# Sums of squares of attention heads: GpSimd's sum over partitions in place of matmuls with ones

## The chip, the cores and the metric

The kernel runs on one core of a Trainium2 chip. A core has five engines with a queue of instructions each: TensorE (PE in the profile, with its weight loads as PEld), VectorE (DVE), ScalarE (ACT), GpSimd (POOL) and SyncE (SP), which issues most of the transfers. Each engine works through its own queue in order and waits on semaphores for the others. SBUF is the memory on the chip, in 128 partitions; TensorE writes its results to PSUM. The metric is the device time of one execution in microseconds (us), the lower the better.

## The reference

One inference step of one layer, on 512 frames of a new stream (prompt) and 64 frames of a running stream with 512 cached frames. All is float32. Cut to what the change touches:

```python
def hybrid_layer(x, k_past, v_past, conv_past, g_norm1, w_in, g_q, g_k, ...):
    hn = rmsnorm(x, g_norm1)
    proj = hn @ w_in                        # D_MODEL = 2048
    q, k, v, gb, gc, hc = jnp.split(proj, ...)
    q = rmsnorm(q.reshape(B, T, N_HEADS, HEAD_DIM), g_q)    # 8 heads x 128 channels
    k = rmsnorm(k.reshape(B, T, N_HEADS, HEAD_DIM), g_k)
    ...
    o_attn = stick_breaking_blocks(q, k_all, v_all, P)
    ...                                     # short gated convolution
    mix = jnp.concatenate([rmsnorm(o_attn, g_attn_out), rmsnorm(o_conv, g_conv_out)], axis=-1)
    x = x + mix @ w_out
    ...                                     # second norm, gated FFN (5632 wide), residual

def stick_breaking(q, k, v, q_pos, k_pos):
    z = jnp.einsum('bqhd,bkhd->bhqk', q, k) / math.sqrt(HEAD_DIM)
    mask = (k_pos[None, :] < q_pos[:, None])[None, None]
    log_1mb = jnp.where(mask, jax.nn.log_sigmoid(-z), 0.0)
    after = lax.cumsum(log_1mb, axis=3, reverse=True) - log_1mb
    w = jnp.where(mask, jnp.exp(jax.nn.log_sigmoid(z) + after), 0.0)
    return jnp.einsum('bhqk,bkhd->bqhd', w, v)
```

`rmsnorm` divides by the root of the mean square. For q and k that mean goes over the 128 channels of one head.

## The kernel before

Channels lie on the partitions and the 576 frames on the free axis, worked on in two halves of 288. A float32 product is made of three fast products: each operand is split into a high part (a copy in the fast type, by ScalarE) and a low part (the difference, by VectorE; `split`, L220 to L222). A projection of 128 columns is 2 halves x 16 steps x 3 matmuls of 128x288.

The time is spent in four stages: the start (x is turned, up to about 45 us), the eight heads (to about 455 us), the convolution groups and the output projection, and the FFN, which takes most. In the stage of the heads each head has three projections (q, k, v), and the attention of the head before is fitted between their steps. The order on TensorE is written out by hand: generators are put on a heap (`Pipeline`), every step of a product is one tick, and `yield n` means "n ticks later". In the heads SP's order is by hand too; VectorE, ScalarE and GpSimd get theirs from a planner, which works with costs of its own.

`norm_evac` (L618) is the normalization of one head's q or k. `evac` runs as soon as a half of the projection lies in PSUM: VectorE scales it to `E` (L636), ScalarE squares it to `sq` (L639), and both split the squares into two parts (L221, L222). 13 ticks later (16 for k; 10 and more in head 0) `rest` lets TensorE multiply both parts by a matrix of ones: `channel_sums` (L467), two matmuls of 128x288 (L469, L470), which give `ss`, in each partition the sum over all partitions, in a PSUM bank called misc. `rsqrt_mean` (L455) makes the reciprocal root of it: `ms` (L460, VectorE reads `ss`), logarithm and exponential by ScalarE (L461, L462), three instructions of VectorE for a step of refinement (L463 to L465). L628 gives `qf` or `kf`, which is split to `qh`, `ql`, `kh`, `kl`. `attend` (L663) starts 15 ticks after the `rest` of k's last half, with the scores (L679, L682) in the banks `z`; then softplus, the mask, the sums of the blocks, and later the products with triangular ones (L725 to L740) and with v (L749). `cz` (L765 to L768) and `os` (L779) are the same for the cached part.

GpSimd does small work beside it: the product with the 0/1 mask `m01` (L691) or `s01` (L754), two additions of blocks per head (L694, L699), one copy and three additions for the cached part (L758, L760), the addition of a head's squares to `acc_a` (L509), and the low part of one weight (L175). In the first output stage it forms differences for `head_forms` (L557) and issues the stores of `mix` (L524).

Of the kernel before, what the change touches and what calls it, by code (L numbers as in the profile page):

```python
# [3 lines left out]

# [6 lines left out]
F32 = mybir.dt.float32  # L11
F32R = mybir.dt.float32r
AF = mybir.ActivationFunctionType
ALU = mybir.AluOpType
PSUM = bass.MemoryType.PSUM

P = 128
TP = 512
TS = 64
# [75 lines left out]
def tile_hybrid_stream_step(  # L95
# [88 lines left out]
    def split_weight(lo_eng):  # L184
        raw = raws[len(ready)]
        n = specs[len(ready)][1] * specs[len(ready)][2]
        hi, lo = weight_split(len(ready))
        for a in range(0, n, 1024):
            weight_parts(raw, hi, lo, a, a + 1024, lo_eng)
# [3 lines left out]
    def next_weight():  # L193
        i = pos[0]
        pos[0] += 1
        end = first_out if i < first_out else first_block
        while len(raws) < min(i + 2, end):
            load_weight()
        while len(ready) < min(i + 2, end):
            split_weight(nc.gpsimd if i == 2 else nc.vector)  # L200
        while len(raws) < min(i + 3, end):
            load_weight()
        out = ready[i]
        ready[i] = None
        return out
# [18 lines left out]
    def parts(name):  # L224
        t = tmp.tile([P, 2, HALF], F32R, tag="hl", name=name)
        return t[:, 0], t[:, 1]
# [273 lines left out]
            else:  # L500
                defer.append((evac, ps, a, b))

    def add_squares(acc, src, first):
        if first:
            nc.scalar.activation(out=acc, in_=src, func=AF.Square)
        else:
            sq = tmp.tile([P, HALF], F32, tag="sq", name="sqm")
            nc.scalar.activation(out=sq, in_=src, func=AF.Square)
            nc.gpsimd.tensor_tensor(out=acc, in0=acc, in1=sq, op=ALU.add)  # L509

    turns = {}

# [105 lines left out]
    def norm_evac(name, gcol, dst_f, dst_hi, dst_lo, first, after=None):  # L618
        E = t1.tile([P, T], F32, tag="E", name=f"E{name}", bufs=2)

        def rest(a, b, sh, sl):
            if first:
                lags[0] += 4
            yield 6 + lags[0] if first else 16 if after else 13
            ss = channel_sums(sh, sl, a, b, "ss")
            r = tmp.tile([P, HALF], F32, tag="r", name="r")
            rsqrt_mean(r, ss, P, HALF)
            nc.vector.scalar_tensor_tensor(out=dst_f[:, a:b], in0=E[:, a:b], scalar=gcol, in1=r,  # L628
                                           op0=ALU.mult, op1=ALU.mult)
            e = min(b, TP)  # L630
            split(dst_hi[:, a:e], dst_lo[:, a:e], dst_f[:, a:e])
            if after and b == T:
                pipe.spawn(after)

        def evac(ps, a, b):
            nc.vector.tensor_tensor(out=E[:, a:b], in0=ps, in1=R1[:, a:b], op=ALU.mult)  # L636
            sq = tmp.tile([P, HALF], F32, tag="sq", name="sq")
            sh, sl = parts("sq")
            nc.scalar.activation(out=sq, in_=E[:, a:b], func=AF.Square)  # L639
            split(sh, sl, sq)  # L640
            pipe.spawn(rest(a, b, sh, sl))

        return evac

# [14 lines left out]
        nc.vector.scalar_tensor_tensor(out=dst, in0=ps, scalar=0.0, in1=scratch, op0=ALU.max, op1=ALU.add)  # L659

    kw = dict(start=False, skip_group_check=True)

    def attend(h, st):  # L663
        yield 15 + (9 if h == 0 else 0)
# [19 lines left out]
        for b in (2, 1, 0):  # L684
            parts = (2, 3) if b == 2 else (b,)
            w = full[b]
            for i in parts:
                scores(i)
            softplus(pr[b][:, :w], z[b][:, :w], pr[b][:, :w])
            for i in parts:  # L690
                nc.gpsimd.tensor_tensor(out=pb[i][:, :P], in0=pb[i][:, :P], in1=m01, op=ALU.mult)  # L691
            split(ph[b][:, : width[b]], pl[b][:, : width[b]], pr[b][:, : width[b]])
            if b == 2:
                nc.gpsimd.tensor_tensor(out=pb[2][:, P:], in0=pb[2][:, P:], in1=pb[3], op=ALU.add)  # L694
                s1h = t1.tile([P, 256], F32R, tag="s1h", name="s1h")
                s1l = t1.tile([P, 256], F32R, tag="s1l", name="s1l")
                split(s1h, s1l, pb[2])
            if b == 1:
                nc.gpsimd.tensor_tensor(out=pb[1][:, P:], in0=pb[1][:, P:], in1=pb[2], op=ALU.add)  # L699
                s0h = t1.tile([P, 384], F32R, tag="s0h", name="s0h")  # L700
                s0l = t1.tile([P, 384], F32R, tag="s0l", name="s0l")
                split(s0h, s0l, pb[1])
# [48 lines left out]

        sp = t1.tile([P, T], F32, tag="pr0", name="sp")
        softplus(sp[:, :320], zc, sp[:, :320])
        nc.gpsimd.tensor_tensor(out=sp[:, 256:320], in0=sp[:, 256:320], in1=s01, op=ALU.mult)  # L754
        sh = t1.tile([P, T], F32R, tag="ph0", name="sph")
        sl = t1.tile([P, T], F32R, tag="pl0", name="spl")
        sums = sp[:, 320:]
        nc.gpsimd.tensor_copy(sums[:, 192:256], sp[:, 256:320])  # L758
        for b in (2, 1, 0):
            nc.gpsimd.tensor_tensor(out=sums[:, b * TS : (b + 1) * TS], in0=sums[:, (b + 1) * TS : (b + 2) * TS],  # L760
                                    in1=sp[:, (b + 1) * TS : (b + 2) * TS], op=ALU.add)
        split(sh, sl, sp)
        yield 18
# [16 lines left out]
        nc.scalar.copy(out=o_attn[h][:, TP:], in_=os_[:, TS:P])  # L780
        for a, b in HALVES:
            yield 3
            add_squares(acc_a[:, a:b], o_attn[h][:, a:b], h == 0)

    def values(h, st, Ev):
        yield 5
# [831 lines left out]
    acc = {}  # L1618
# [226 lines left out]
```

## Time and profile before

| what | us |
|---|---|
| median of 3 runs | 2382.36 (2382.0 to 2385.2) |
| profiled execution, first to last instruction | 2383.4 |
| TensorE busy in it | 2361.4 (99%) |
| VectorE busy | 1919.3 (81%) |
| ScalarE busy | 1172.1 (49%) |
| GpSimd busy | 295.2 (12%) |

The page gives the profiled execution no other time than its span, which lies within the range of the runs. Times inside a profile count from the span's start. In the lines below, `L212 PE MATMUL pj<-x,whi` is an instruction of line 212 on TensorE that writes `pj` and reads `x` and `whi`. A row of the timeline begins with start and duration; behind it stands, in brackets, how long the engine was idle before and what released it. A row of groups by form gives busy time, mean nanoseconds of one, and the idle time ahead of the group. A row of waits gives the total, the number of times and the longest. Matmuls overlap in the engine, so the starts of neighbours tell what one of them costs, not its duration. Some matmul records can be missing.

### The profile page before, as it was taken

What the parts mean: (1) busy time and instruction counts of PE and PEld (TensorE: products, weight loads), DVE (VectorE), ACT (ScalarE), POOL (GpSimd) and SP (SyncE); (2) the same over time, 40 slices, a digit from 0 to 9 for tenths busy, and PEclk for the clock granted to TensorE, in tenths of its full rate; (3) what the DMA queues carried; (4) which work ended last, traced back from release to release, by engine and by line L of the source; (5) the groups of instructions that cost most, each with busy time, mean ns of one, the idle gap of its engine ahead of it and who ended that gap; (6) DMA issues with size and microseconds to landing.
All of it is one profiled execution on the core that took longest, in us unless ns stands there. A gap on an engine that the chain in (4) does not pass through costs nothing.

```text
span 2383.4 us, 44109 instructions
## 1 busy us (share of the span) xinstructions
PE 2361.4 (99%) x17765; PEld 2349.5 (99%) x17765; DVE 1919.3 (81%) x2884; ACT 1172.1 (49%) x2107; POOL 295.2 (12%) x386
## 2 busy tenths in 40 slices
PE   8999999999999999999999999999999999999999
PEld 8999999999999999999999999999999999999999
DVE  7767776688887899888888888888888777887876
ACT  6666665444444555444444444444444444444444
POOL 1111111242111130000000000000000002431211
PEclk9999999999999999999999999999999999999999
DMA  8354433584367745444444444444444936886642
GB/s 257 117 152 142 144 112 96 184 285 127 109 216 199 217 155 177 151 125 147 152 131 143 150 137 140 147 144 134 146 147 133 355 116 207 221 231 198 202 132 81
DMA packets 512260, 390.76 MB, mean 164 GB/s; under 512 B 11838, under 2 KB 501176, under 8 KB 512056
## 3 DMA queue, kind: packets, MB, share of 16 engines
q1 hardware_dynamic: 502712, 371.40, 48.8%
q0 software_dynamic: 8624, 16.22, 3.3%
q8 instruction: 139, 2.28, 0.4%
q14 instruction: 65, 0.53, 0.1%
q10 hardware_dynamic: 720, 0.33, 0.0%
HBM read 298.82 MB, written 89.08 MB: 163 GB/s over the span
## 4 chain that ended last, share of the span: by engine, by line
PE 88%; DVE 5%; DMA 3%; ACT 2%; issue 1%; POOL 0%; SPq 0%; ACTq 0%; DVEq 0%; POOLq 0%
PE psy L1529 34%; PE psw L1529 17%; PE pj L212 11%; PE psx L1529 9%; PE psy L1033 5%; PE pjo L212 4%; PE psw L1033 3%; PE psx L1033 1%; DMA raw_a<-in_w_out_dram 1%; DMA o_ob<-xt_dram 1%; DVE whl L1005 1%; PE z L682 1%; PE po L749 0%; DMA raw_a<-in_w_down_dram 0%; DMA raw_a<-in_w_in_dram 0%
## 5 line engine op out<-in xcount | busy, mean ns | idle before, releaser
L1529 PE MATMUL psy<-h_s,whl 128*128 128x288 f32 x2787 | 411.4, 294 | 0.3 <-ACT part L1539 0.3
L212 PE MATMUL pj<-x,whi 128*128 128x288 f32 x1856 | 398.2, 299 | 0.3 <-DVE x L355 0.3
L1529 PEld LDWEIGHTS psy<-h_s,whl 128*128 128x128 f32 x2787 | 383.5, 188 | 0.6 <-ACT part L1539 0.6
L222 DVE TENSOR_TENSOR whl<-raw_a,whl 128x1024 fp32r<-128x1024 f32 (+4 forms) x296 | 323.1, 1092 | 59.1 <-ACT whl L221 58.3
L1529 PE MATMUL psw<-t,whl 128*128 128x288 f32 x2400 | 348.1, 295 | 0.0
L1529 PEld LDWEIGHTS psw<-t,whl 128*128 128x128 f32 x2400 | 327.7, 188 | 0.0
L221 ACT CAST whl<-raw_a 128x1024 fp32r<-128x1024 f32 (+4 forms) x296 | 267.8, 906 | 114.5 <-issue 35.4
L212 PEld LDWEIGHTS pj<-x,whi 128*128 128x128 f32 x1856 | 306.6, 189 | 1.0 <-DVE x L355 0.6
L212 PE MATMUL pj<-x,wlo 128*128 128x288 f32 x928 | 274.2, 295 | 0.1
L222 DVE TENSOR_TENSOR whl<-raw_b,whl 128x1024 fp32r<-128x1024 f32 (+5 forms) x190 | 200.6, 1056 | 70.4 <-ACT whl L221 69.2
L221 ACT CAST whl<-raw_b 128x1024 fp32r<-128x1024 f32 (+5 forms) x190 | 165.2, 872 | 169.1 <-issue 72.8
L1539 ACT COPY part<-psy 128x288 f32<-128x288 f32 x242 | 96.4, 398 | 282.8 <-PE psy L1529 281.3
L1529 PE MATMUL psy<-b22m,whl 128*128 128x288 f32 x1212 | 182.7, 294 | 0.4 <-ACT part L1539 0.4
L1529 PE MATMUL psy<-t2t,whl 128*128 128x288 f32 x1212 | 183.0, 294 | 0.0
L212 PEld LDWEIGHTS pj<-x,wlo 128*128 128x128 f32 x928 | 174.9, 188 | 0.7 <-DVE wlo L422 0.3
L1529 PE MATMUL psx<-h_s,whl 128*128 128x288 f32 x1185 | 173.5, 294 | 0.0
L1529 PEld LDWEIGHTS psy<-b22m,whl 128*128 128x128 f32 x1212 | 168.0, 188 | 0.7 <-ACT part L1539 0.7
L1529 PEld LDWEIGHTS psy<-t2t,whl 128*128 128x128 f32 x1212 | 168.2, 188 | 0.2 <-DVE whl L222 0.2
L1529 PEld LDWEIGHTS psx<-h_s,whl 128*128 128x128 f32 x1185 | 162.6, 188 | 0.0
L221 ACT CAST whl<-s 128x1024 fp32r<-128x1024 f32 (+5 forms) x81 | 72.3, 892 | 101.5 <-PE psw L1529 101.4
L1308 POOL DMA_DIRECT2D hid_dram<-form x3 | 2.2, 750 | 947.2 <-DVE form L222 947.2
L1529 PE MATMUL psy<-t,whl 128*128 128x288 f32 x576 | 107.6, 296 | 0.0
(483 smaller groups left out, 4446.7 us busy)
## 6 DMA issues: line engine op xcount, KB each, us to landing
hid_dram<-form SPq DMA_DIRECT2D x147, 288.0 KB, 2.3
raw_a<-in_w_in_dram SPq DMA_DIRECT2D x41, 1024.0 KB, 6.5
raw_a<-in_w_gate_dram SPq DMA_DIRECT2D x22, 1024.0 KB, 6.0
raw_a<-in_w_up_dram SPq DMA_DIRECT2D x22, 1024.0 KB, 5.7
raw_b<-in_w_gate_dram SPq DMA_DIRECT2D x22, 1024.0 KB, 6.6
raw_b<-in_w_up_dram SPq DMA_DIRECT2D x22, 1024.0 KB, 7.6
h_s<-hid_dram SPq DMA_DIRECT2D x10, 2016.0 KB, 11.6
raw_a<-in_w_out_dram SPq DMA_DIRECT2D x16, 1024.0 KB, 5.4
```

Source lines behind the costliest of these rows:

```text
L212: mm(ps, w_[:, k, csl], x_, start=(k == 0 and n == 0), stop=(k == nk - 1 and n == 2))
L221: nc.scalar.copy(out=hi, in_=src)
L222: (lo_eng or nc.vector).tensor_tensor(out=lo, in0=src, in1=hi.bitcast(F32), op=ALU.subtract)
L682: mm(zb[i], a_[:, kk], b_[:, q0:TP], start=(n == 0), stop=False, skip_group_check=True)
L1005: tt(out=whl[:, 1], in0=src, in1=whl[:, 0].bitcast(F32), op=ALU.subtract)
L1033: mm(ps, whl[:, w_, j, :], x_, start=(start and j == 0 and q == 0), stop=(j == m - 1 and q == 2), skip_group_check=True)
L1308: q.dma_start(out=hid_dram[fp][2 * n - 2 : 2 * n].rearrange("f p t -> p f t"), in_=t.bitcast(F32))
L1529: mm(ps, whl[:, w_, j, :], x_, start=(start and j == 0 and q == 0), stop=(j == len(xs_) - 1 and q == 2), skip_group_check=True)
L1539: nc.scalar.copy(out=t, in_=st["y"])
```

## The change

Four things are changed, all but one in the stage of the heads.

1. `norm_evac` no longer splits the squares and no longer multiplies by ones. `evac` gives the squares, whole, to GpSimd's `partition_all_reduce`, which writes the sum over the 128 partitions to all of them, in SBUF; `rest` reads it there. The result lies in the buffer (tag `hl`) that the split squares had. The other sums by `channel_sums` (the attention's and the convolution's output norm, the second norm) stay matmuls.
2. The products with the masks become selections by position (`affine_select`) on GpSimd: `later_queries`. For the cached part a `memset` of 64 partitions follows, since `s01` was zero there too.
3. The additions of blocks, of the cached part's sums and of the heads' squares go from GpSimd to VectorE; those of the convolution's squares stay.
4. One weight's low part goes from GpSimd to VectorE.

Counted over the program, TensorE has 64 matmuls less, ScalarE 32 casts less, VectorE 32 subtractions less and 48 other instructions more, and GpSimd 32 sums over partitions, 40 selections and 8 memsets more in place of 88 two-input operations. GpSimd's queue also holds two more special instructions, which switch the code that its cores have loaded: one behind `rst` (L440), ahead of the first sum, and one ahead of the first difference of `head_forms` (L557), behind two stores of `mix`. SP has as many instructions as before.

```diff
-            split_weight(nc.gpsimd if i == 2 else nc.vector)
+            split_weight(nc.vector)
...
-    def add_squares(acc, src, first):
+    def add_squares(acc, src, first, eng=nc.gpsimd):
...
-            nc.gpsimd.tensor_tensor(out=acc, in0=acc, in1=sq, op=ALU.add)
+            eng.tensor_tensor(out=acc, in0=acc, in1=sq, op=ALU.add)
...
-        def rest(a, b, sh, sl):
+        def rest(a, b, ss):
...
-            ss = channel_sums(sh, sl, a, b, "ss")
...
             sq = tmp.tile([P, HALF], F32, tag="sq", name="sq")
-            sh, sl = parts("sq")
             nc.scalar.activation(out=sq, in_=E[:, a:b], func=AF.Square)
-            split(sh, sl, sq)
-            pipe.spawn(rest(a, b, sh, sl))
+            ss = tmp.tile([P, HALF], F32, tag="hl", name="ss")
+            nc.gpsimd.partition_all_reduce(ss, sq, P, bass_isa.ReduceOp.add)
+            pipe.spawn(rest(a, b, ss))
...
+    def later_queries(t, base):
+
+        nc.gpsimd.affine_select(out=t, in_=t, compare_op=ALU.is_ge, fill=0.0, base=base,
+                                pattern=[[1, t.shape[1]]], channel_multiplier=-1)
...
-                nc.gpsimd.tensor_tensor(out=pb[i][:, :P], in0=pb[i][:, :P], in1=m01, op=ALU.mult)
+                later_queries(pb[i][:, :P], -1)
...
-                nc.gpsimd.tensor_tensor(out=pb[2][:, P:], in0=pb[2][:, P:], in1=pb[3], op=ALU.add)
+                nc.vector.tensor_tensor(out=pb[2][:, P:], in0=pb[2][:, P:], in1=pb[3], op=ALU.add)
...
-                nc.gpsimd.tensor_tensor(out=pb[1][:, P:], in0=pb[1][:, P:], in1=pb[2], op=ALU.add)
+                nc.vector.tensor_tensor(out=pb[1][:, P:], in0=pb[1][:, P:], in1=pb[2], op=ALU.add)
...
-        nc.gpsimd.tensor_tensor(out=sp[:, 256:320], in0=sp[:, 256:320], in1=s01, op=ALU.mult)
+        later_queries(sp[:, 256:320], TS - 1)
+        nc.gpsimd.memset(sp[:TS, 256:320], 0.0)
...
-            nc.gpsimd.tensor_tensor(out=sums[:, b * TS : (b + 1) * TS], in0=sums[:, (b + 1) * TS : (b + 2) * TS],
+            nc.vector.tensor_tensor(out=sums[:, b * TS : (b + 1) * TS], in0=sums[:, (b + 1) * TS : (b + 2) * TS],
...
-            add_squares(acc_a[:, a:b], o_attn[h][:, a:b], h == 0)
+            add_squares(acc_a[:, a:b], o_attn[h][:, a:b], h == 0, nc.vector)
```

More of the change, by code (lines that the diff above doesn't have):

```diff
@@ L5 @@
 import concourse.bass as bass
+import concourse.bass_isa as bass_isa
 import concourse.tile as tile
```

## The prediction

> **What bounds the kernel now.** I read the head of the page and the chain first, then a window over steady heads, then the two matmuls that go, and then who waits for whom there.
>
> ```profile
> span 2383.4 us, 44109 instructions
> PE 2361.4 (99%) x17765; PEld 2349.5 (99%) x17765; DVE 1919.3 (81%) x2884; ACT 1172.1 (49%) x2107; POOL 295.2 (12%) x386
> ...
> PE 88%; DVE 5%; DMA 3%; ACT 2%; issue 1%; POOL 0%; SPq 0%; ACTq 0%; DVEq 0%; POOLq 0%
> ...
> 90.00:405.00 315.00, 314.02 (x2336) 310.17 (x2336) 225.83 (x442) 191.70 (x413) 48.63 (x92) 1.00 0.42 128
> ...
> 114.07 1.22 PE z L682 x6
> ...
> 413.54 1.23 PE z L682 x6
> ```
>
> TensorE holds 88% of the chain and is busy 314.02 of 315 us in the window (its columns: PE, weight load, VectorE, ScalarE, GpSimd, then clock and DMA). The clock is 1.00, so nothing is to be had there. The two score rows lie six heads apart: (413.54 - 114.07)/6 = 49.9 us per head. Per head VectorE is busy 225.83 x 49.9/315 = 35.8 us and GpSimd 48.63 x 49.9/315 = 7.7 us. So a matmul taken out of TensorE's row is worth its issue interval, as long as VectorE's 14.1 idle us per head are not used up.
>
> ```profile
> 105.74 0.29 PE L469 MATMUL ss<-sq,oner 128*128 128x288 f32 x1
> 105.87 0.29 PE L470 MATMUL ss<-sq,oner 128*128 128x288 f32 x1
> 106.00 0.30 PE L212 MATMUL pj<-x,whi 128*128 128x288 f32 x1
> ...
> PE z L682 <- ACT kh L221: 1.6, 3, 0.8
> PE kc L800 <- ACT zc L710: 1.0, 1, 1.0
> PE kc L800 <- DVE ms L460: 0.5, 1, 0.5
> PE ss L469 <- DVE ms L460: 0.3, 1, 0.3
> ```
>
> A matmul is shown as 0.29 us but the next one starts 0.13 us later: the pair takes 106.00 - 105.74 = 0.26 us of the row. Between 40 and 480 us TensorE waits for other engines 3.4 us in all: only the scores' wait for kh, in 3 heads of 8, repeats.
>
> **Part 1: the matmuls go.** 8 heads x (q, k) x 2 halves = 32 pairs at 0.262 us (0.131 each) = 8.4 us off TensorE. The wait of ss for a free bank (0.3) and of kc behind it (0.5) hang on the bank that ss held: they go, 0.8 us. What is late next is the scores; I leave their 1.6 us. The gain passes to the end if what follows is tied to the heads' end, not to the clock:
>
> ```profile
> 457.72 0.14 PE ssg L469
> ...
> 518.31 8.63 DMA raw_a<-in_w_in_dram
> ```
>
> After the last head the chain goes from ssg through VectorE's scaling to this load, each released by the one before, so it moves forward as a block.
>
> **Part 2: the splits and the additions.** The rows of 47 to 420 us, by form:
>
> ```profile
> L222 DVE TENSOR_TENSOR sq<-sq 128x288 fp32r<-128x288 f32 x32 | 17.8, 559 | 3.7 <-ACT sq L221 3.5
> ...
> L606 DVE TENSOR_TENSOR o_ob<-o_ob 128x288 f32<-128x288 f32 x8 | 3.6, 454 | 0.1
> ...
> L719 DVE SCALAR_TENSOR_TENSOR z<-z,acA 128x128 f32<-128x128 f32 x28 | 8.3, 295 | 7.0 <-PE z L728 6.2 <-PE z L734 0.6
> ...
> L222 DVE TENSOR_TENSOR pl<-pr,ph 128x256 fp32r<-128x256 f32 x15 | 6.7, 448 | 1.5 <-ACT ph L221 1.5
> ...
> L772 DVE SCALAR_TENSOR_TENSOR ws<-ws,acA 128x64 f32<-128x64 f32 x7 | 1.5, 214 | 0.0
> ...
> L175 DVE TENSOR_TENSOR wlo<-raw_a,whi 128x1024 fp32r<-128x1024 f32 x43 | 52.4, 1225 | 6.8 <-ACT whi L174 6.4
> ```
>
> VectorE loses 17.8 us of subtractions. It gains 14 x 0.454 = 6.4 (the head squares' additions), 8 x 0.295 = 2.4 and 8 x 0.448 = 3.6 (block sums), 24 x 0.214 = 5.1 (the cached part's sums) and 2 x 1.225 = 2.5 (a weight's low part): 20.0, so +2.2 in all, or 0.3 per head, beside 14.1 idle. ScalarE loses 32 casts and gains nothing. Both hidden; without cover the 2.2 us would be the price. GpSimd's masks become one-input selections; the two rows of such at the start are first below, and an addition of GpSimd follows that part 3 needs:
>
> ```profile
> L246 POOL TENSOR_SCALAR_AFFINE_SELECT acA<-acA 128x128 f32<-128x128 f32 x1 | 0.3, 292 | 0.0
> ...
> L251 POOL TENSOR_SCALAR_AFFINE_SELECT acA<-acA 128x64 f32<-128x64 f32 x1 | 0.2, 239 | 0.0
> ...
> L509 POOL TENSOR_TENSOR acc_a<-acc_a,sqm 128x288 f32<-128x288 f32 x14 | 12.5, 890 | 85.4 <-ACT sqm L508 85.4
> ```
>
> **Part 3: the sum over partitions, X us each.** No row shows it. Below: it is a sum over a 128x288 tile, so hardly under the same engine's addition of that shape, 0.89 (last row). A tree over 128 partitions has 7 halvings: 7 x 0.89 = 6.2. I take the geometric middle, the root of 0.89 x 6.2 = 2.35. Far end: one partition after another; a column of one pass costs (292 - 239)/64 = 0.83 ns, so 288 x 128 x 0.83 = 30.6 us. Its place in a head:
>
> ```profile
> 201.27 0.44 ACT L639 ACTIVATE sq<-Ek 128x288 f32<-128x288 f32 x1 [0.34 <-DVE Ek L636]
> ...
> 208.33 0.45 DVE L460 TENSOR_SCALAR ms<-ss 128x288 f32<-128x288 f32 x1
> ...
> 212.21 0.39 DVE L222 TENSOR_TENSOR kl<-kf,kh 128x224 fp32r<-128x224 f32 x1 [0.45 <-ACT kh L221]
> ...
> 213.50 0.28 PE L682 MATMUL z<-qh,kh 128*128 128x256 f32 x1
> ```
>
> This is the head's last half, the one that the scores wait for. The squares are ready at 201.71, and ms used its sum only at 208.33: 6.6 us cover X = 2.35 here. The new wait is at ms on VectorE. Behind it in the changed order stand, in head 0, both subtractions of a weight that is used one projection later, elsewhere the rest of the normalization and x's sums; in a head in which ms stands straight after Eq, VectorE stands still for about 0.45 + 2.35 us, out of 14.1. On GpSimd the cached part's mask may stand behind a sum and be X late, but its three additions leave GpSimd. SP's DMAs are the same in number; POOL's two mix stores come ahead of the second code switch.
>
> **Part 4: two switches of GpSimd's code.** The changed order holds two more special instructions: after rst, and before the head forms' first subtraction. Bounds: between the ends of the memset and the start of the selection below lay one such instruction and 0.08 us; above, a transfer of 1 MB takes 6.5 us to land.
>
> ```profile
> 0.81 0.20 POOL masks.py:197 MEMSET ident<- 128x128 f32 x1 [0.29 <-POOLq L1832]
> ...
> 1.09 0.29 POOL masks.py:199 TENSOR_SCALAR_AFFINE_SELECT ident<-ident 128x128 f32<-128x128 f32 x1
> ...
> raw_a<-in_w_in_dram SPq DMA_DIRECT2D x41, 1024.0 KB, 6.5
> ...
> 38.78 1.21 POOL L440 TENSOR_TENSOR rst<-ssr,nhalf 128x5 f32<-128x5 f32 x1 [12.09 <-DVE ssr L438]
> ...
> 47.02 0.81 ACT L639 ACTIVATE sq<-Eq 128x288 f32<-128x288 f32 x2 [6.86 <-DVE Eq L636]
> ...
> 465.06 0.74 POOL L524 DMA_DIRECT2D mix_dram<-mx  x1 [7.33 <-DVE mx L522]
> ...
> 468.66 1.78 POOL L557 TENSOR_TENSOR o_oa<-o_oa 128x288 f32<-128x288 f32 x2 [2.86 <-DVE hf L222]
> ...
> 476.18 2.29 POOL L557 TENSOR_TENSOR o_oa<-o_oa 128x288 f32<-128x288 f32 x2 [1.50 <-DVE hf L222]
> ...
> 485.75 2.24 POOL L557 TENSOR_TENSOR o_ob<-o_ob 128x288 f32<-128x288 f32 x2 [3.04 <-DVE hf L222]
> ```
>
> The first has 47.4 - 40.0 = 7.4 us of cover, more than 6.5. The second has 2.9; the upper bound would start the subtractions 3.6 late, which GpSimd's idle 1.50 and 3.04 later in that chain take up. I take 0 for both and keep 3.6 for the range.
>
> **Sum.** -8.4 - 0.8 = -9.2 us. The page gives the profiled execution no time but its span, 2383.4, which is 1.0 above the runs' median of 2382.4; nothing else lies around it. So 2374.2 against the span, 2373.2 against the median. Changes within 0.2%, 4.8 us (2377.6 to 2387.2), are what a measurement of this kernel can hardly tell from none.
>
> **Rival 1, slower: VectorE is shut out while GpSimd sums.**
>
> ```profile
> 49.51 5.00 POOL L175 TENSOR_TENSOR wlo<-raw_a,whi 128x1024 fp32r<-128x1024 f32 x2 [9.53 <-ACT whi L174]
> ...
> 50.99 0.46 DVE L460 TENSOR_SCALAR ms<-ss 128x288 f32<-128x288 f32 x1 [1.98 <-PE ss L470]
> ...
> 52.44 2.38 DVE L463 TENSOR_TENSOR t<-y 128x288 f32<-128x288 f32 x1 [0.20 <-ACT y L462]
> ```
>
> While GpSimd's two additions run (49.51 to 54.51), VectorE's product of two SBUF inputs lasts 2.38 us and ends 0.3 after them; the one that reads PSUM takes its usual 0.46. If the sums shut VectorE out for all of X, a head needs 35.8 + 0.3 + 4X of VectorE against TensorE's 49.9 - 1.05 = 48.9. It decides from X = 3.2. At 2.35 a head needs 45.5 and the gain stands; at 4 it needs 52.1, so 8 x 2.2 = 17.6 us more than before: 2400; at 6.2, 60.9: +88, 2470. Against it: products that read PSUM go on, and 7.7 us of GpSimd's present two-input work shut VectorE out already and shrink to some 2. The Trainium skill (SBUF — State Buffer, section "SBUF: two separate sides") says that the pair of ports is an exclusive lock, taken for the whole instruction; the row above agrees, and no run yet shows whether a sum over partitions holds it to its end. Chance 0.20, for X between 3.2 and 6.2.
>
> **Rival 2, much slower: the sums walk the partitions one by one and GpSimd is the bound.** From X = 12 on (48.9/4) GpSimd alone exceeds the head; at the far end 4 x 30.6 = 122 us per head, 8 x 72.5 = +580: 2962. The Trainium skill (GPSIMD Engine Reference, section 3.2, Cross-partition) has 247.7 us for a reduction along partitions of a 128x2048 tile; scaled to 288 columns that would be an estimate of 34.8 us each. Against it: it is another instruction than the one used. No row decides; 0.05.
>
> **Rival 3, no change: the scores eat the gain.** If kh and kl are ready no earlier than now, TensorE reaches the scores 0.52 us sooner per head (two pairs lie between) and waits for it: 8 x 0.52 = 4.2 lost, and 3.6 by the second switch. Gain 9.2 - 7.8 = 1.4: 2381. For it: kl ends at 212.60, 0.9 before the scores, and three heads wait already. Against it: the 6.6 us of cover above. 0.14.
>
> **Chances.** Forecast 0.56 (faster; own range 2371, with the scores' 1.6 us as well, to 2377). No change 0.14. Slower 0.30: rival 1 0.20, rival 2 0.05, and 0.05 for orders of VectorE that stall on ms for more than the idle time. The range goes from 2371 to 2400, rival 1 at X = 4; rival 2 and the upper half of rival 1 stay out.
>
> **What would show it.** Right: 64 fewer matmuls on ss, per-head distance of the score rows near 48.9, sums over partitions under 3.2 us, ms waiting little, TensorE still at 99%. Wrong: VectorE rows of two SBUF inputs that last as long as the sum beside them, TensorE waiting for kh or for whi/wlo in each head, a sum over 3.2 us, GpSimd idle before the first sum until after 48 us, or the head forms' subtractions starting late.

## The result, and the profile after

The changed kernel takes 2394.43 us (median of 5 runs, 2394.02 to 2400.26) against 2384.19 (2382.0 to 2385.94) for the kernel before in the same series: a ratio of 1.0045, 95% interval 1.0034 to 1.0057. It is 10 us (0.45%) slower, where 9 us less was forecast; the range of 2371 to 2400 holds it, on the other side of zero. (A correction to the count under "The change": VectorE has 56 other instructions more, not 48, and GpSimd has lost 96 two-input operations, not 88.)

The head of the page and its chain, of the changed kernel:

```profile
span 2392.7 us, 43956 instructions
PE 2360.4 (99%) x17701; PEld 2348.3 (98%) x17701; DVE 1917.9 (80%) x2908; ACT 1166.2 (49%) x2075; POOL 325.2 (14%) x370
...
PE 86%; DVE 5%; DMA 3%; ACT 2%; POOL 2%; issue 1%; SPq 0%; ACTq 0%; POOLq 0%; DVEq 0%
```

The 64 matmuls are gone, and still TensorE's busy time fell by 1.0 us instead of 8.4, while the span grew by 9.3. So TensorE both waits and runs slower than before. Where it waits, from 20 to 620 us (us in total, times, longest), in the changed kernel:

```profile
PE os L785 <- issue: 7.2, 4, 2.7
PE psy L1039 <- ACT whl L1008: 3.1, 1, 3.1
...
PE vta L648 <- DVE Ev L835: 2.0, 1, 2.0
PE cz L772 <- DVE spl L223: 1.6, 3, 0.7
PE cz L771 <- ACT sph L222: 1.4, 1, 1.4
```

At vta TensorE turns v, so that its frames lie on the partitions; psy is a product of the stage after the heads. These 15.3 us are new. The old waits of the heads (z, kc and ss, 3.4 us together) have all but gone, and one of 1.5 us behind the heads. The windows of the changed kernel that are slower than before (columns as in the prediction: stretch, length, TensorE, weight load, VectorE, ScalarE, GpSimd, clock, DMA share, GB/s):

```profile
45.00:90.00 45.00, 42.71 (x309) 41.72 (x308) 36.08 (x67) 25.26 (x53) 13.62 (x10) 0.96 0.51 154
240.00:290.00 50.00, 46.76 (x329) 46.00 (x329) 32.68 (x66) 25.92 (x55) 9.47 (x12) 0.93 0.40 121
...
265.00:270.00 5.00, 5.00 (x24) 5.00 (x23) 1.08 (x3) 0.65 (x2) 0.00 (x0) 0.51 0.55 157
500.00:550.00 50.00, 45.17 (x316) 44.09 (x314) 36.89 (x49) 20.82 (x33) 16.02 (x21) 0.93 0.83 273
```

The clock, 1.00 in all of these before, is 0.96, 0.93 and 0.93. Behind the longest wait of os, which ends at 263.85, TensorE runs at half clock until about 270: 24 matmuls in five microseconds, where at 0.131 us each some 38 fit. There are three such stretches at half clock: 65.15 to 68.56, 263.12 to 269.95 and 515.71 to 522.53 us, 17.1 us in all, which cost about half of that, 8.5 us. The heads of the two pages close the account: TensorE's idle time grew from 22.0 to 32.3 us, by 10.3; of the 8.4 us of matmuls that went, its busy time shows only 1.0, so the clock took 7.4 back (the rest of the 8.5 lies in the waits themselves). 10.3 - 1.0 = 9.3, the growth of the span.

What makes the waits. The group of the sums, and VectorE's longest wait between 45 and 470 us, in the changed kernel:

```profile
L640 POOL PARTITION_ALL_REDUCE ss<-sq x32 | 73.0, 2287 | 149.9 <-ACT sq L638 146.3 <-DVE ms L461 3.6
```

```profile
DVE ms L461 <- POOL ss L640: 35.6, 21, 2.6
```

A sum takes 2.29 us; 2.35 was estimated. The price of the unknown instruction was right, and the loss came all the same. The tail of head 1 on GpSimd, VectorE and TensorE in the changed kernel (start, duration; in brackets the idle time before and what ended it):

```profile
146.10 3.00 POOL L640 PARTITION_ALL_REDUCE ss<-sq  x1 [5.09 <-ACT sq L638]
...
148.99 0.31 POOL L665 TENSOR_SCALAR_AFFINE_SELECT sp<-sp 128x64 f32<-128x64 f32 x1
...
149.83 0.23 DVE L766 TENSOR_TENSOR sp<-sp 128x64 f32<-128x64 f32 x1 [2.56 <-POOL sp L764]
...
155.26 1.23 DVE L176 TENSOR_TENSOR wlo<-raw_a,whi 128x1024 fp32r<-128x1024 f32 x1
...
155.79 2.54 POOL L640 PARTITION_ALL_REDUCE ss<-sq  x1 [5.99 <-ACT sq L638]
...
158.36 0.31 DVE L461 TENSOR_SCALAR ms<-ss 128x288 f32<-128x288 f32 x1 [1.87 <-POOL ss L640]
...
160.09 0.48 DVE L777 TENSOR_TENSOR ws<-cz,zc 128x320 f32<-128x320 f32 x1
...
161.68 1.13 PE L785 MATMUL os<-ws,cV 128*128 128x128 f32 x8 [1.72 <-issue]
```

and the same place in the kernel before:

```profile
155.04 0.48 DVE L771 TENSOR_TENSOR ws<-cz,zc 128x320 f32<-128x320 f32 x1
...
156.06 0.47 ACT L774 ACTIVATE ws<-ws 128x320 f32<-128x320 f32 x1 [2.20 <-DVE ws L772]
...
159.61 1.05 PE L779 MATMUL os<-ws,cV 128*128 128x128 f32 x8
```

Two things stand out. The weights `ws` of the cached part, which TensorE needs for os, stand on VectorE behind ms of k's last half, and ms waits 1.87 us for a sum. And before that VectorE stands still for 2.56 us at the cached part's additions, because on GpSimd their mask stood behind the sum of k's first half. (The profile names no releaser for os, "issue"; it starts 0.1 us after ScalarE's exponential of ws, which ends at 161.58.) So ws comes 160.09 - 155.04 = 5.05 us later, 1.5 of it a lag from before, since the scores of head 1 start at 114.41 instead of 112.92; and in the kernel before ws was ready 159.61 - 156.53 = 3.1 us ahead of os. The room at this place is 3.1 us, not the 14.1 us per head of the prediction.

Last, GpSimd's second code switch, in the changed kernel:

```profile
472.18 0.74 POOL L525 DMA_DIRECT2D mix_dram<-mx  x1 [8.20 <-DVE mx L523]
481.50 3.07 POOL L558 TENSOR_TENSOR o_oa<-o_oa 128x288 f32<-128x288 f32 x3 [8.59 <-issue]
```

In the kernel before, 2.86 us lay between the store and this subtraction. 8.59 us are more than the upper bound taken for the switch (6.5). The head forms come late, whl with them, TensorE waits 3.1 us at psy, and the clock falls. The first switch is hidden, as forecast.

### The profile page after: what moved, and what is told of

Same layout as the page of the kernel before. It is cut to its first block, busy times and chain, and to the rows that moved or that the text cites. A ratio compares the mean times of both kernels' runs of the same rounds, so it can differ in the third digit from the quotient of the medians.

```text
span 2392.7 us, 43956 instructions
## 1 busy us (share of the span) xinstructions
PE 2360.4 (99%) x17701; PEld 2348.3 (98%) x17701; DVE 1917.9 (80%) x2908; ACT 1166.2 (49%) x2075; POOL 325.2 (14%) x370
## 4 chain that ended last, share of the span: by engine, by line
PE 86%; DVE 5%; DMA 3%; ACT 2%; POOL 2%; issue 1%; SPq 0%; ACTq 0%; POOLq 0%; DVEq 0%
PE psy L1535 34%; PE psw L1535 17%; PE psx L1535 9%; PE pj L213 8%; PE psy L1039 6%; PE pjo L213 4%; PE psw L1039 3%; PE psx L1039 2%; POOL ss L640 1%; DMA form_dram<-hf 1%; DVE wlo L176 1%; PE os L785 0%; PE z L687 0%; DMA raw_a<-in_w_down_dram 0%; DMA xs_dram<-xs_out 0%
```

## The experiments

All times are medians of series with the kernel before on the same chip, which came out at 2384.4 to 2385.8 us there. The series ran on five chips, so times of different series are set against the kernel before in the table further down.

### The moves without the sums

```diff
-            nc.gpsimd.partition_all_reduce(ss, sq, P, bass_isa.ReduceOp.add)
+            split(sh, sl, sq)          # and ss = channel_sums(sh, sl, a, b, "ss") in rest
```

> The sums over partitions are taken by the two matmuls with ones again; the selections in place of the masks and all additions moved to VectorE stay. Theory of the queue order (the loss comes from VectorE standing still at ms for GpSimd's sum with ws behind it, from the TensorE clock after the pauses that this makes, and from the code switch before the head forms): all three need the sums, so the time is the kernel before's within 0.2% (2380 to 2388), os waits under 0.5 us in all, the clock stays at 1.00 between 45 and 600 us, and the head forms' first addition on GpSimd starts within 1 us of before's 468.66. Rival (the moved additions cost VectorE and delay the path): 2388 or more, with waits of TensorE for VectorE in the heads.

Measured: 2383.51 us, ratio 0.9993 (0.9985 to 1.0002). os waits no more, the clock is 1.00 in every window. The selections and the additions moved to VectorE cost nothing: the loss hangs on the sums, and on the code switches that come with them.

### The order at ms, and the code switch

`ws_first` shortens the delay ahead of cz; `early_switch` puts a small product behind the last sum; the third does both.

```diff
-        yield 18
+        yield 14 if h else 18
         cz = misc("cz")
...
-        yield 16
+        yield 20 if h else 16
         os_ = misc("os")
```

```diff
             nc.gpsimd.partition_all_reduce(ss, sq, P, bass_isa.ReduceOp.add)
+            if name == "k" and h_now[0] == NH - 1 and b == T:
+                nc.gpsimd.tensor_tensor(out=nhalf[:, 4:5], in0=ss[:, 0:1], in1=nhalf[:, 3:4], op=ALU.mult)
```

> All 32 sums stay on GpSimd. From head 1 on the four matmuls of cz are issued 8 projection matmuls (1.05 us) earlier, which puts ws and its exponential ahead of ms of k's last half on VectorE and ScalarE; nothing else moves. Theory of the queue order: os no longer waits (7.2 us in the changed kernel, now under 1), the fall of the clock at 264 us (2.8 us) goes; cz may wait up to 1 us more per head for the split of sp, where it waited already (3.0 us in 4 heads). So 3 to 10 us less than the changed kernel: 2384 to 2391. The wait of vta and the late head forms stay. Rival (GpSimd's sums shut VectorE out by the shared ports, whatever the order): os still waits, or the scores do, and the time stays at 2392 to 2397.

> The changed kernel with one more GpSimd product of 128x1 (a spare column, read by nobody) right behind the last sum of the last head, so that GpSimd changes its code back there, some 45 us before the head forms need it. Theory: the 8.6 us that GpSimd stood idle ahead of the head forms' first addition was the code switch, so it starts 1 to 3 us after the mix store instead (before: 2.86), near 476; whl comes in time, psy's wait of 3.1 us and the slow clock from 515 to 523 go: 4 to 7 us less than the changed kernel, 2387 to 2391. The 8.6 us appear as idle time after that product. Rival (the addition was late for another reason, the mix store or VectorE's split): it starts at 481 again and the time stays at 2394.

> Both edits together. If the two causes are separate and each is named rightly, their gains add: 7 to 16 us less than the changed kernel, 2378 to 2387, and what is left of the loss against the forecast is vta's wait of 2.0 us with its slow clock (1.6 us) and the waits of cz. If the causes overlap (the pauses are one delay that is only moved), the gain is that of the larger one alone.

Measured: ws_first 2396.1 us (1.0046, 1.0034 to 1.0058), no gain. TensorE's waits in it, 20 to 620 us:

```profile
PE cz L772 <- DVE spl L223: 7.1, 7, 1.4
...
PE cz L771 <- ACT sph L222: 3.0, 4, 1.4
```

os waits no more, but cz, 1.05 us earlier, waits just as long for the split of sp. The edit moved the wait instead of removing it; VectorE was late before it came to ms at all. That is the theory's first miss: the standstill at ms with ws behind it is not the whole cause.

early_switch: 2391.34 us (1.0033, 1.0020 to 1.0045), 3.1 us less than the 2394.43 of the changed kernel, a little short of the 4 to 7 expected (4.1 us, when each is taken against the kernel before of its own series). GpSimd in it:

```profile
409.24 2.53 POOL L641 PARTITION_ALL_REDUCE ss<-sq  x1 [4.67 <-ACT sq L639]
419.57 0.18 POOL L643 TENSOR_TENSOR nhalf<-ss,nhalf 128x1 f32<-128x1 f32 x1 [7.80 <-issue]
...
475.63 1.79 POOL L558 TENSOR_TENSOR o_oa<-o_oa 128x288 f32<-128x288 f32 x2 [3.15 <-DVE hf L223]
```

The 7.80 us now lie where GpSimd has nothing else to do, the first subtraction waits 3.15 us for VectorE as it did before, psy's wait of 3.1 us is gone and the clock from 500 to 550 us is 1.00. This part of the loss is shown. (The slow stretch behind os at 264 us is gone too, though os waits as before; the last section shows why that is chance.) Both together gave 2392.74 (1.0031, 1.0020 to 1.0042): as early_switch alone. All later kernels with sums have the early switch.

### No sum

```diff
-            nc.gpsimd.partition_all_reduce(ss, sq, P, bass_isa.ReduceOp.add)
+            nc.gpsimd.tensor_copy(ss, sq)
```

> The sum over partitions is left out: GpSimd copies the squares in its place (0.3 to 0.9 us instead of 2.3), so the normalization divides by the wrong thing; everything else, order included, is the changed kernel. No change of GpSimd's code is needed. Theory of the sum's duration (VectorE waits at ms, and GpSimd's mask of the cached part waits behind a sum; both pass to TensorE as waits of os and cz): with X near 0.4 us the waits of ms shrink from 35.6 us to under 10, os and cz wait under 1 us together, and the forecast's gain appears: 2385.2 - 9 = 2376, within 2373 to 2379. Rival (what costs is the order of the instructions or the additions on VectorE, whatever the sum lasts): 2388 or more.

Measured: 2371.58 us (0.9950, 0.9938 to 0.9963), 4 us below the 2376 expected and below the range; of the old waits of the heads only 0.9 us is left, at the scores. VectorE's wait at ms, which was 35.6 us:

```profile
DVE ms L461 <- POOL ss L640: 7.6, 16, 1.0
```

The forecast's gain is there when what GpSimd does lasts 0.75 us. The order alone and the moves are not the cause: 19 to 20 us lie between this kernel and early_switch, and the sum is what differs. (VectorE's order hardly does: of 756 instructions up to the attention's output norm 8 stand elsewhere than in the changed kernel.)

### Which sums: k's first half, k's second half, only q's

```diff
+            if after and a == 0:
+                two = parts("sq")
+                split(*two, sq)
+                pipe.spawn(rest(a, b, None, two))
+                return
```

This is k1_matmul; `rest` then calls `channel_sums(*two, a, b, "ss")`. In k2_matmul the condition is `after and b == T`, in q_only `after`; in these two the early product reads the last `Ek`.

> The early code switch, and the first half of k summed by matmuls again; 24 sums stay on GpSimd. Theory that GpSimd's queue is the second cause: k's first sum is what the cached part's mask stood behind (at 148.99 us in the changed kernel, ready at 146.3), so VectorE's idle time at the cached part's additions (2.56 us in head 1) goes, sph and spl come 2 us earlier and the waits of cz (3.0 us) go. In this kernel's order ws also stands ahead of ms of k's last half, so os waits little. From early_switch's 2391.3: -7.2 (os) - 3.0 (cz) + 8 pairs x 0.262 = 2.1: 2383, within 2380 to 2386.

> The early code switch, and the last half of k summed by matmuls again; 24 sums stay on GpSimd, among them k's first half ahead of the cached part's mask. ws stands ahead of ms in this order too. If GpSimd's queue (mask behind sum) is a cause of its own, cz still waits 3 us or more, while os waits under 1: 2391.3 - 7.2 + 2.1 = 2386, within 2384 to 2389, some 3 us above the kernel with k's first half by matmuls. If only the standstill at ms counts, both come out alike.

> The early code switch, and both halves of k summed by matmuls; the 16 sums of q stay on GpSimd. q's first use is the scores, a projection later than k's second half, so neither ws nor the cached part's mask stands behind a sum: no waits of os, and of cz no more than before. The moves alone measured 2383.5; less 16 pairs x 0.262 = 4.2 us: 2379, within 2377 to 2382, the first time below the kernel before. Rival (any sum on GpSimd costs VectorE its ports, wherever it stands): 2385 or more.

Measured: 2380.26 us (0.9984, 0.9975 to 0.9993), 2386.35 (1.0012, 1.0003 to 1.0020) and 2381.27 (0.9988, 0.9979 to 0.9996), all within the expected times, though the 6 us between the first two are more than the 3 expected. TensorE's waits of the heads, k1_matmul and then k2_matmul:

```profile
PE vta L658 <- DVE Ev L846: 2.5, 2, 2.3
...
PE os L795 <- issue: 1.1, 1, 1.1
...
PE cz L782 <- DVE spl L223: 0.5, 1, 0.5
```

```profile
PE ss L471 <- DVE sq L223: 3.7, 5, 0.9
PE ss L470 <- ACT sq L222: 3.0, 2, 2.0
```

The sum of k's first half is the dear one: without it 24 sums give a gain, with it the wait only moves on, from os to ss (6.7 us), and not to cz as expected. In all three kernels the planner also puts ws ahead of ms of k's last half from head 1 on; that is no difference among them, but it is one against early_switch. At this point the cached part's mask, which stands behind just this sum on GpSimd, looked like the second cause.

### The mask off GpSimd

```diff
-        later_queries(sp[:, 256:320], TS - 1)
-        nc.gpsimd.memset(sp[:TS, 256:320], 0.0)
+        nc.vector.tensor_tensor(out=sp[:, 256:320], in0=sp[:, 256:320], in1=s01, op=ALU.mult)
...
-        nc.gpsimd.tensor_copy(sums[:, 192:256], sp[:, 256:320])
+        nc.vector.tensor_copy(sums[:, 192:256], sp[:, 256:320])
```

> The early code switch; all 32 sums stay on GpSimd and the order of ms and ws stays the changed kernel's. The cached part's mask is one product of 128x64 on VectorE and its copy of 128x64 goes to VectorE too, so that nothing of the cached part stands behind a sum on GpSimd. If the mask behind the sum is a cause of its own: VectorE's idle time at the cached part's additions (7.1 us with ms behind it) and the waits of cz (3.0 us) go, and os waits less than 7.2 us, as VectorE comes earlier to the standstill at ms: from early_switch's 2391.3 to 2383 to 2388. If it is the standstill at ms alone: 2390 or more, os still 7 us.

> mask_on_vector, and cz 8 projection matmuls earlier from head 1 on, so that ws stands ahead of ms on VectorE; all 32 sums still on GpSimd. With both queues mended cz no longer waits for spl in spite of its earlier place (in ws_first that wait, 7.1 us, ate the gain) and os does not wait. 2391.3 - 3.0 - 7.2 = 2381, within 2378 to 2384; what is left against no_sum's 2371.6 is the first head (vta, 2 us, and its slow clock) and the ports. If the two queues are not what it is: 2386 or more.

Measured: 2389.71 us (1.0019, 1.0010 to 1.0028) and 2391.66 (1.0027, 1.0017 to 1.0037). Both missed: 1.6 us less than early_switch, and nothing. Mending both queues does not mend the time. What else stands in the way, in the timeline of mask_on_vector:

```profile
188.00 3.40 DVE L176 TENSOR_TENSOR wlo<-raw_a,whi 128x1024 fp32r<-128x1024 f32 x2
...
188.14 2.91 POOL L641 PARTITION_ALL_REDUCE ss<-sq  x1 [8.27 <-ACT sq L639]
...
196.21 1.97 POOL L641 PARTITION_ALL_REDUCE ss<-sq  x1 [4.07 <-ACT sq L639]
196.22 1.53 DVE L629 SCALAR_TENSOR_TENSOR qf<-Eq,gqs,r 128x288 f32<-128x288 f32 x1
```

VectorE's instructions of two SBUF inputs are stretched beside the sums: the two low parts take 3.40 us (2.40 before), the product qf, which takes 0.51 elsewhere, takes 1.53. That is Rival 1's mechanism, which I had set aside by then. Taking the mask out of GpSimd's queue does not touch it: in the mean the low parts take 1.33 us and qf 0.64 us here as in early_switch. Nor did it end the wait: VectorE no longer waits for the mask (5.0 us in early_switch), but it waits 36.7 us at ms instead of 35.6, and os still waits 6.5 us.

### Wait or ports

By the ports I mean what Rival 1 described: VectorE's instructions of two SBUF inputs last longer while GpSimd sums. Four kernels part the wait at ms from the ports. In the first two GpSimd copies the squares instead of summing them, twice or three times over; in the other two it copies them once for ms, and then sums them for nobody.

```diff
-            nc.gpsimd.partition_all_reduce(ss, sq, P, bass_isa.ReduceOp.add)
+            nc.gpsimd.tensor_copy(ss, sq)
+            nc.gpsimd.tensor_copy(ss.bitcast(mybir.dt.bfloat16).rearrange("p (a b) -> p a b", a=2),
+                                  sq[:, None, :].to_broadcast([P, 2, HALF]))
```

```diff
-            nc.gpsimd.partition_all_reduce(ss, sq, P, bass_isa.ReduceOp.add)
+            nc.gpsimd.tensor_copy(ss, sq)
+            nc.gpsimd.partition_all_reduce(sq, sq, P, bass_isa.ReduceOp.add)
```

In longer_wait_no_sum the last copy stands twice; sum_unread_mask_on_vector has the mask's edit above as well.

> The sum over partitions is left out: GpSimd copies the squares in its place, twice, first 288 and then 576 columns of 128 rows. In no_sum a copy of 288 columns took 0.75 us and VectorE's subtraction of a weight's low part beside it 1.24 (1.22 in the kernel before), so that the pair lasts about 2.25 us, as long as the sum, and leaves VectorE its ports. No change of GpSimd's code. If VectorE's wait at ms is what costs, the time stays near early_switch's: 2388 to 2392, and os waits 5 us or more. If it is the ports, the time falls to 2378 or less, near no_sum's 2371.6. In between, the two share the loss by where it falls.

> The use of the sum is left out: GpSimd first copies the squares to where ms reads (0.75 us) and then sums them over partitions in place, for nobody; the early code switch. So GpSimd is busy, and VectorE's ports are held, as in early_switch or longer, while ms waits for the copy alone. If VectorE's wait at ms is what costs: near no_sum's 2371.6, below 2378. If it is the ports, or GpSimd's queue: 2386 or more.

> As same_wait_no_sum, whose two copies lasted 0.69 + 0.75 = 1.44 us together and so less than the sum, with a third copy of 576 columns: some 2.2 us, and VectorE's waits at ms from 25.5 to about 40 us (35.6 with the sums). The sum is left out. If the wait at ms costs by itself, the time rises by more than the copy's 8 x 0.75 us of a head's tail, to 2384 or more, with os waiting; if it is the ports, it stays at 2374 to 2379.

> sum_unread with the cached part's mask and copy on VectorE, so that nothing but a copy of squares (0.77 us) stands on GpSimd in anybody's way, and what the sums do to others they do through the ports alone. The use of the sum is left out. If it is the ports: within 3 us of sum_unread, 2386 to 2392, os still waiting 3 us or more. If sum_unread lost its time in GpSimd's queue (VectorE waited 11.0 us for the mask's copy there): 2380 or less.

Measured: 2374.29 us (0.9951, 0.9939 to 0.9964), 2391.44 (1.0024, 1.0014 to 1.0035), 2381.97 (0.9984, 0.9975 to 0.9993) and 2386.36 (1.0003, 0.9994 to 1.0012). The first two fit the ports (or, the second, GpSimd's queue), the third came out between its two expectations, the fourth at the ports' lower edge. VectorE's wait in longer_wait_no_sum, and TensorE's wait of os in it:

```profile
DVE ms L461 <- POOL ss L642: 28.3, 21, 2.5
```

```profile
PE os L787 <- issue: 3.3, 4, 1.7
```

VectorE's wait in same_wait_no_sum, in which os does not wait:

```profile
DVE ms L461 <- POOL ss L641: 25.5, 25, 1.7
```

and VectorE's and TensorE's waits in sum_unread_mask_on_vector:

```profile
DVE ms L461 <- POOL ss L641: 9.5, 16, 2.6
```

```profile
PE vta L652 <- DVE Ev L839: 3.8, 2, 3.2
PE os L788 <- issue: 3.3, 2, 2.2
```

Put together. The second column of times is against the kernel before of the same series. The last two are from each kernel's profiled execution: when the first head's scores start, and the time from there to the last start of the last head's (`z<-qh,kh`).

| what is left of the sum | us | against before | first scores | to the last head's |
|---|---|---|---|---|
| no_sum: 7.6 us of wait at ms | 2371.6 | -12.8 | 67.0 | 333.4 |
| same_wait_no_sum: 25.5 us of wait, no ports held by a sum | 2374.3 | -11.6 | 68.9 | 334.0 |
| longer_wait_no_sum: 28.3 us of wait, no ports held by a sum | 2382.0 | -3.2 | 69.0 | 340.6 |
| sum_unread_mask_on_vector: ports, 9.5 us of wait | 2386.4 | +1.2 | 73.8 | 339.8 |
| sum_unread: ports and GpSimd's queue, 10.4 us of wait | 2391.4 | +5.6 | 76.2 | 341.9 |
| mask_on_vector: ports and 36.7 us of wait | 2389.7 | +4.5 | 70.9 | 347.6 |
| early_switch: all three, 35.6 us of wait | 2391.3 | +6.1 | 71.9 | 348.7 |

By the whole times the parts do not add up: with ports and queue there, shortening the wait from 35.6 to 10.4 us seems to bring nothing (2391.4 against 2391.3). Behind the first head they nearly do. Against no_sum's 333.4 us the wait costs 7.2 there, the ports 6.4, the ports with GpSimd's queue 8.5 (so the queue some 2.1), wait and ports together 14.2, and all three 15.3; 7.2 + 6.4 + 2.1 is 15.7. So each has its part in the loss, the wait and the ports about alike (GpSimd's queue alone was not tried). What hides this is the first head: the two kernels with the unread sum, in which GpSimd is busy some 0.7 us longer per half for the copy, reach its scores 6.8 and 9.2 us after no_sum, early_switch only 4.9.

Three reserves. These are single executions, that of sum_unread the fastest of its eight (2388.09), and between first and last scores longer_wait_no_sum, sum_unread_mask_on_vector and mask_on_vector each have a stretch of 3.4 us at half clock, 1.7 us of loss, the others none. longer_wait_no_sum is not the wait alone: its three copies keep GpSimd busy 2.60 us per half, longer than a sum, and VectorE's low parts take 1.28 us in the mean instead of 1.22. And the planner orders anew: of VectorE's 756 instructions some 35 stand elsewhere than in the changed kernel in the two kernels with the unread sum, 67 in same_wait_no_sum and 124 in longer_wait_no_sum; what that alone does was not tried.

The total of the wait does not decide: 25.5 us in 25 pieces of at most 1.7 us cost 0.6 us behind the first head, 28.3 us in 21 pieces of at most 2.5 us cost 7.2. That fits a threshold, a wait that still fits into the room of the tail and one that does not, but with the reserves above it is not shown, and where it lies was not tried.

### A version that beats both

```diff
-            if after and a == 0:
+            if first or (after and a == 0):
```

> k1_matmul with all four sums of the first head by matmuls as well (21 sums on GpSimd). In the first head the waits of vta (2.5 us) and of the scores (1.6 us) follow the standstills at ms; 3 pairs of matmuls more cost 0.8. 2380.3 - 2.5 - 1.6 + 0.8 = 2377, within 2375 to 2380; if those waits have another cause, 2381.

Measured: 2377.81 us (0.9967, 0.9955 to 0.9979), as expected. 21 sums stay on GpSimd: 7 heads, both halves of q and the last of k. vta waits no more, the scores wait 0.2 us, and the clock is 1.00 in every window up to the FFN.

## Why the prediction was wrong

- **Part 1, the matmuls:** right. 64 fewer, and the moves together with a short instruction in the sum's place (no_sum) are 12.8 us faster than the kernel before; the old waits go with the matmuls, more of them than the 0.8 us counted.
- **Part 2, the additions:** right, hidden (moves_only).
- **Part 3, X:** right in size, 2.29 against 2.35, and by luck: behind 2.35 stood only the middle between two bounds a factor of seven apart.
- **Part 3, the cover: the step that failed.** "In a head in which ms stands straight after Eq, VectorE stands still ... out of 14.1." Idle time of a whole head was set against a standstill at one place. The list of what stands behind ms left out `ws`, which os needs, and that place has 3.1 us of room. VectorE stood still 35.6 us at ms, 4.5 per head and far below 14.1, and TensorE waited all the same (os 7.2 us, cz 3.0). The 6.6 us of cover were looked up for the scores, and the scores indeed never became late (0.2 us of wait). "The cached part's mask may stand behind a sum and be X late" was written down and not followed to its reader, which stands still for 2.56 us.
- **Rival 1:** the mechanism was named, its price and its point were wrong. It was made to decide from X = 3.2, by summing VectorE's time over a head. Measured, the ports add little to VectorE's time in total; the groups of the changed kernel (45 to 460 us; busy time, mean ns) and below them qf before:

```profile
L176 DVE TENSOR_TENSOR wlo<-raw_a,whi 128x1024 fp32r<-128x1024 f32 x50 | 66.3, 1335 | 8.9 <-ACT whi L175 8.2
...
L628 DVE SCALAR_TENSOR_TENSOR qf<-Eq,gqs,r 128x288 f32<-128x288 f32 x16 | 10.2, 640 | 0.3
```

```profile
L628 DVE SCALAR_TENSOR_TENSOR qf<-Eq,gqs,r 128x288 f32<-128x288 f32 x16 | 8.2, 512 | 0.0
```

The low parts took 1.225 us before, so 50 x 0.11 = 5.5 us, and qf 16 x 0.128 = 2.0: about 1 us per head. The ports cost time nonetheless, at X = 2.29: some 6 us in the seven later heads by the table above. That they do so because they fall into the same tail is argued, not shown. The Trainium skill (SBUF — State Buffer, section "SBUF: two separate sides") has a VectorE instruction with two SBUF inputs fully blocked by a GpSimd instruction that started first, for the whole of it. The trace agrees in kind: qf took 1.53 us beside a sum. It differs in degree: qf, started at 196.22, ended at 197.75, 0.43 us before the sum (196.21 + 1.97 = 198.18); since the profile's spans on GpSimd are rough, that alone is weak. And the sums are stretched themselves, from 1.97 us to 2.5 and 3.0 beside VectorE's work.
- **Part 4, the switches:** the upper bound of 6.5 us was a transfer's time and not a bound: GpSimd stood idle 6.9 to 8.7 us around a switch in the kernels here. "GpSimd's idle 1.50 and 3.04 later in that chain take up" the delay did not hold; moving the switch brought 3 to 4 us.
- **"The clock is 1.00, so nothing is to be had there":** true, but there was something to lose. New pauses of TensorE were followed by 17.1 us at half clock, and no term of the sum had that.
- **Rivals 2 and 3:** refuted, by X and by the scores. The 0.05 for "orders of VectorE that stall on ms for more than the idle time" was the case nearest to what happened. That the range holds 2394 is luck: its upper end was Rival 1 at X = 4.

## What to carry to other kernels

An engine's idle time per loop covers nothing by itself: follow the queue behind the instruction that will wait, to the first reader on the engine that bounds, and compare the delay with the room at that reader (here 3.1 us, not 14.1). Work that leaves a bounding engine for GpSimd comes with three prices that fall on VectorE at the same spot: the wait for it, what stands behind it in GpSimd's own queue, and the ports; put it where no reader is near (q's sums and k's last half), and leave the rest where it was. Where GpSimd must load other code, let it do so early, by a small instruction at a place where it has nothing to do.

## What was not expected of the hardware

TensorE's clock fell after short pauses, and not after each of them. The end of the same wait of os in the changed kernel and in early_switch, and below them windows of 3.41 us around it in both (changed kernel first; the clock is the third column from the right):

```profile
263.85 2.05 PE L785 MATMUL os<-ws,cV 128*128 128x128 f32 x8 [2.73 <-issue]
```

```profile
265.14 1.13 PE L788 MATMUL os<-ws,cV 128*128 128x128 f32 x8 [2.73 <-issue]
```

```profile
259.71:263.12 3.41, 1.42 (x11) 1.18 (x9) 2.59 (x6) 0.89 (x2) 0.79 (x1) 1.00 0.00 0
263.12:266.54 3.42, 2.69 (x12) 2.72 (x13) 2.06 (x6) 1.03 (x3) 0.00 (x0) 0.50 0.00 0
266.54:269.95 3.41, 3.41 (x16) 3.41 (x15) 0.46 (x1) 0.47 (x2) 0.00 (x0) 0.50 0.79 226
```

```profile
260.68:264.09 3.41, 1.73 (x14) 1.49 (x12) 2.26 (x5) 0.89 (x2) 1.11 (x1) 1.00 0.00 0
264.09:267.51 3.42, 2.37 (x19) 2.40 (x20) 2.57 (x8) 1.51 (x4) 0.00 (x0) 1.00 0.02 7
```

A pause of 2.73 us is followed by a clock of 0.50 in the one and of 1.00 in the other; eight matmuls of os take 2.05 us and 1.13 us. The windows tell why. In every profile here the clock changes only at moments that lie a whole number of 3.41 us apart, and the windows above are cut at these. In the changed kernel 2.0 us of the pause fall into one window (3.41 - 1.42), and the next one is slow; in early_switch the pause is split, 1.7 and 1.05 us, and the clock stays. So it was in all the runs: a window at full clock in which TensorE had no matmul for 1.9 us or more was followed by half clock each time, one with less than 1.49 us never, and between 1.49 and 1.85 both happened. The threshold is thus near half a window, and where a pause lies on the grid is luck. Five profiles, no_sum among them, have a slow stretch near 900 us, in the FFN, which the change does not touch: 1.7 us that say nothing about it.

The Trainium skill (TensorE: Matmul & The Clock Gate, section "What's actually happening") has the clock halved after an idle window of about 3.4 us that runs free of the program. That the same pause counts once and not another time agrees with a free-running window; that 1.9 us of 3.41 were enough does not agree with a window that has to be idle throughout.

A sum over the 128 partitions of a 128x288 tile takes 1.97 us undisturbed, in this case a little more than two additions of that shape on the same engine (0.89 each), and not the 30.6 us estimated for a walk from partition to partition. Its code has to be loaded, and so has that of the next two-input operation afterwards: the records of the changed kernel show, behind the start, a switch at 41.2 and at 473.0 us and none between, where selections, memsets and copies stand among the sums.
